# An output projection in scaled fp16 pairs, prepared a block of 256 tokens ahead

## The chip, the cores and the metric

The kernel runs on one core of one Trainium2 chip. The metric is the device time of one execution in microseconds (us).

## What is computed

One hybrid encoder layer is applied to two batches, of 4096 and of 1024 tokens, with a width of 1024. RMSNorm and one combined projection feed three branches (a long convolution through an FFT, dilated attention over three windows, and cross-attention into a memory); the branches are concatenated, gated and projected. The change concerns the last line, and the loads of its weights:

```python
z = h @ w_in                                   # h = rms_norm(x), w_in 1024 x 3584
y_hy  = x0 * (conv + s * skip)                 # 384 channels
y_att = sum over three windows of softmax-weighted outputs   # 384 channels
y_mem = memory_attention(...)                  # 256 channels
mixed = concat([y_hy, y_att, y_mem]) * silu(gate)
return x + mixed @ w_out                       # w_out 1024 x 1024, f32
```

The matrix products want more than one 16-bit or reduced pass: each f32 operand is split into a high and a low part, and three products (high by high, high by low, low by high) are added in PSUM.

## The kernel before, in words

The work is written as one Python class on top of a tile framework. The order on TensorE is the order in which the program issues it; on the other engines (VectorE, ScalarE, GpSimd and the SP queue, which issues all DMAs) the framework's scheduler chooses the order from priorities and dependencies when the kernel is built. Each engine then runs its list in order, so an instruction that waits holds all behind it.

- First the channels of the convolution are projected, and its filter made. Then two streams are woven on TensorE: `dense` projects q, k and v (`qkv`, tile by tile of 128 tokens) and later the gates (`gates`, matmuls `zg`); `side` runs the long convolution, the memory branch and the attention.
- While `qkv` runs its second half it takes one step of the generator `gate_prep` (L1166) before each tile, 18 steps in all. In the kernel before `gate_prep` has eight: each loads 128 columns of the gate's weights into the tile `ws` (one buffer, tag `gws`), scales and splits them with `wsplit`, and stores them to `wgd`. `long_conv` runs meanwhile; its first stage (`conv_stage1`) reads a PSUM tile `a` (two buffers) with ScalarE and VectorE, which write the pair `av` (VectorE's part is L1294); four such pairs make one store `as_d`.
- The output comes last, after the gates. `out_weights` (L1428) loads `w_out` in eight pieces `wos` and splits each into `wo`: a rounded fp32r copy by ScalarE (L1434) and the remainder by VectorE (L1435).
- `output` (L1437) works through 20 blocks of 256 tokens, each of two tiles of 128. `hy(n)` loads the convolution's parts (`hc`, `hs`, `hx`) and the gate `gg` of a block, applies Silu (L1456), the skip (L1459, VectorE) and two products on GpSimd (L1462, L1464) to give `mxh`. `merge(n, t)` loads one tile's three attention outputs `y` (the tile y3, two buffers) and the memory output into `ya` (two buffers), and merges the three by their softmax denominators: small VectorE operations `md` and `mw` (L1483 to L1494), one Exp on ScalarE (L1488), products on VectorE and GpSimd (L1497, L1501), and the sum `ya` (L1504).
- `mixed(k)` (L1512) makes one tile's operand: TensorE transposes `ya` in five pieces into two PSUM tiles `ot` (tag f, three buffers, L1525), VectorE multiplies by the gate into `mm` (L1526), ScalarE rounds `mm` and `mxh` to fp32r into `mhi` (L1529, L1531), and VectorE (L1530) and GpSimd (L1532) subtract to give `mlo`.
- The loop at the end of `output` runs over 40 tiles. Each takes two halves of 512 columns; for each half `mm3` (L277, matmuls at L282 to L284) issues 24 matmuls into the PSUM tile `oo` (two buffers), which VectorE adds to the residual `xr` (L1553). The transposes for tile k+1 stand ahead of tile k's matmuls, `merge` for tile k+2 is issued in the same step.

```python
nc.tensor.matmul(out, pick_l(lh, k), pick_r(rh, k), start=(k == 0), stop=False)
nc.tensor.matmul(out, pick_l(lh, k), pick_r(rl, k), start=False, stop=False)
nc.tensor.matmul(out, pick_l(ll, k), pick_r(rh, k), start=False, stop=(k == n - 1))
```

Of the kernel before, what the change touches and what calls it, by code (L numbers as in the profile page):

```python
# [150 lines left out]
XR = 4  # L151
# [30 lines left out]
class Layer:  # L182
# [983 lines left out]
    def gate_prep(self, pool):  # L1166

        self.wgd = self.dram.tile([P, 8, KC * 2 * P], F16, name="wgd")
        self.Sg = self.const.tile([P, 8], F32, name="Sg")
        for j in range(8):  # L1170
# [3 lines left out]
            yield  # L1174

# [252 lines left out]
    def out_weights(self, pool, lpool):  # L1428
        nc, x = self.nc, self.x
        self.wo = wo = pool.tile([P, KC, 2, DM], F32R, name="wo", bufs=1)  # L1430
        for k in range(KC):
            w = lpool.tile([P, DM], F32, tag="xr", name="wos", bufs=XR)
            self.ld(w, x["w_out"][0][k * P:(k + 1) * P, :])
            nc.scalar.activation(out=wo[:, k, 0], in_=w, func=AF.Copy)  # L1434
            nc.vector.tensor_tensor(out=wo[:, k, 1], in0=w, in1=wo[:, k, 0].bitcast(F32), op=ALU.subtract)  # L1435

    def output(self, lpool, rpool, ps):  # L1437
# [29 lines left out]
        def merge(n, t):  # L1467
# [42 lines left out]
        todo = [(n, t) for n in range(len(blocks)) for t in range(B // P)]  # L1510
        pend = {0: hy(0)}
        ms = {0: merge(0, 0), 1: merge(0, 1)}  # L1512

        def mixed(k):
            n, t = todo[k]
            g, mxh = pend[n]
            ya, xr = ms.pop(k)
            ts = slice(t * P, (t + 1) * P)
            hi = rpool.tile([P, KC, P], F32R, tag="mhi", name="mhi", bufs=2)
            lo = rpool.tile([P, KC, P], F32R, tag="mlo", name="mlo", bufs=2)  # L1520
            mm = rpool.tile([P, 5, P], F32, tag="mm", name="mm", bufs=2)
            for c0, nchunk in ((0, 4), (4, 1)):
                tp = ps.tile([P, 4, P], F32, tag="f", name="ot", bufs=3)
                for c in range(nchunk):
                    nc.tensor.transpose(tp[:, c, :], ya[:, (c0 + c) * P:(c0 + c + 1) * P], self.ident)  # L1525
                nc.vector.tensor_tensor(  # L1526
                    out=mm[:, c0:c0 + nchunk], in0=tp[:, :nchunk], in1=g[:, 3 + c0:3 + c0 + nchunk, ts], op=ALU.mult
                )
            nc.scalar.activation(out=hi[:, 3:8], in_=mm, func=AF.Copy)  # L1529
            nc.vector.tensor_tensor(out=lo[:, 3:8], in0=mm, in1=hi[:, 3:8].bitcast(F32), op=ALU.subtract)  # L1530
# [145 lines left out]
```

## Time and profile before

| | |
|---|---|
| time, median of 3 runs | 3075.26 us (3065.23 to 3078.64) |
| time of the profiled execution | 3081.23 us |
| its span, first to last instruction | 3079.5 us |
| mean granted TensorE clock | 0.973 of full speed |
| TensorE busy | 2780.3 us, 90% |
| VectorE, ScalarE, GpSimd busy | 67%, 54%, 43% |
| share of the DMA engines' time | 73% |
| the output's matmuls `oo` | 1920 matmuls, first at 2593.9 us, last at 3074.8 us |

PE is TensorE, PEld its weight loads, DVE VectorE, ACT ScalarE, POOL GpSimd, SPq the queue of SyncE. All times are from the start of the span. A busy share is no limit by itself: TensorE's matmuls overlap, so their pace is read from the distance of their starts.

### The profile page before, as it was taken

To read this page: it belongs to the slowest core of one execution; us is meant where nothing else is said; L and a number is where in the kernel's file an instruction comes from. 1 tells how busy PE (TensorE), PEld (TensorE's weight loads), DVE (VectorE), ACT (ScalarE), POOL (GpSimd) and SP (SyncE) were. 2 spreads that over 40 slices of the span, in tenths; PEclk is the share of its full clock that TensorE was granted. 3 is DMA by queue.
4 is the path that set the end of the run, shared out by engine and by line. 5 is a ranking of instruction groups with operands and counts; after the bars stand their busy time and mean duration, and the time that the engine had idled before them with its cause. 6 is when DMAs were issued, how large, how long until landed. Compare 5 with 4: busy or idle time off the path is not lost. (4 is left out here: it accounts for less than half of the span.)

```text
span 3079.5 us, 55518 instructions
## 1 busy us (share of the span) xinstructions
PE 2780.3 (90%) x19620; PEld 1727.0 (56%) x19620; DVE 2072.2 (67%) x5239; ACT 1667.0 (54%) x3147; POOL 1338.5 (43%) x1574
## 2 busy tenths in 40 slices
PE   5998888988999997987998999998898899999999
PEld 2444444433544444543456666676666665778877
DVE  7777888788668761463668767676667666766663
ACT  5666666334779863472336666565565564323321
POOL 2336777243246651252424333333243344655551
PEclk9999999999999998998999999999999999999999
DMA  7654444545589866685589999998998979777762
GB/s 221 176 154 148 151 153 147 160 154 189 213 227 241 217 178 178 219 180 135 156 192 261 227 204 229 210 226 177 199 220 195 202 175 309 252 245 256 237 219 103
DMA packets 761953, 610.79 MB, mean 198 GB/s; under 512 B 514814, under 2 KB 702358, under 8 KB 758218
## 3 DMA queue, kind: packets, MB, share of 16 engines
q1 hardware_dynamic: 761674, 607.23, 73.4%
q8 instruction: 155, 2.54, 0.3%
q14 instruction: 124, 1.02, 0.1%
HBM read 289.08 MB, written 200.32 MB: 159 GB/s over the span
## 5 line engine op out<-in xcount | busy, mean ns | idle before, releaser
L1067 ACT ACTIVATE pt<-pt,nm 128x256 f32<-128x256 f32 (+2 forms) x880 | 349.8, 472 | 177.0 <-DVE nm L1065 170.2
L282 PE MATMUL z<-wA,hA 128*128 128x512 f16 (+1 forms) x960 | 353.9, 369 | 35.9 <-DVE vr L476 23.3
L284 PE MATMUL z<-wA,hA 128*128 128x512 f16 (+1 forms) x960 | 353.4, 368 | 0.0
L283 PE MATMUL z<-wA,hA 128*128 128x512 f16 (+1 forms) x960 | 353.1, 368 | 0.0
L1055 DVE CUSTOM_DVE_ANT_0 pt<-s,tab,lsc 128x256 f32<-128x256 f32 (+1 forms) x672 | 277.3, 448 | 84.6 <-PE s L1051 74.6
L282 PE MATMUL zh<-hB,wh 128*128 128x512 f16 x720 | 279.2, 388 | 24.4 <-ACT zb L879 24.2
L283 PE MATMUL zh<-hB,wh 128*128 128x512 f16 x720 | 278.8, 387 | 1.5 <-DVE hB L387 1.5
L284 PE MATMUL zh<-hB,wh 128*128 128x512 f16 x720 | 278.9, 387 | 0.0
L282 PE MATMUL oo<-wo,mhi 128*128 128x512 f32 x640 | 257.2, 402 | 8.9 <-ACT mhi L1531 3.6
L284 PE MATMUL oo<-wo,mlo 128*128 128x512 f32 x640 | 253.9, 397 | 0.3 <-POOL mlo L1532 0.3
L283 PE MATMUL oo<-wo,mhi 128*128 128x512 f32 x640 | 253.8, 396 | 0.0
L282 PE MATMUL zg<-hG,wg 128*128 128x512 f16 x640 | 246.0, 384 | 0.0
L284 PE MATMUL zg<-hG,wg 128*128 128x512 f16 x640 | 245.8, 384 | 0.0
L283 PE MATMUL zg<-hG,wg 128*128 128x512 f16 x640 | 245.7, 384 | 0.0
L1083 POOL CAST hl<-pt 128x256 f16<-128x256 f32 (+1 forms) x212 | 104.7, 508 | 312.0 <-ACT pt L1067 238.2
L1103 DVE TENSOR_TENSOR tl<-tt,th 128x512 f16<-128x512 f32 (+1 forms) x280 | 187.7, 672 | 56.7 <-ACT th L1102 55.2
L1102 ACT ACTIVATE th<-tt 128x512 f16<-128x512 f32 (+1 forms) x280 | 160.1, 574 | 115.0 <-PE yp L1124 55.0
L1048 PE MATMUL s<-kT,qT 128*128 128x256 f16 (+2 forms) x720 | 165.8, 261 | 42.0 <-DVE mx L1055 40.8
L1098 PE MATMUL tt<-ident,pt 128*128 128x128 f32 x1088 | 172.3, 280 | 31.3 <-DVE tl L1103 25.2
L1338 ACT ACTIVATE kt<-kp,rn 64x384 f32<-64x384 f32 x328 | 188.0, 573 | 12.8 <-PE kp L1332 7.6
L1084 POOL TENSOR_TENSOR hl<-pt,hl 128x256 f16<-128x256 f32 (+1 forms) x212 | 191.6, 911 | 6.8
L893 DVE SCALAR_TENSOR_TENSOR u<-zb,cw,u 128x512 f32<-128x512 f32 (+2 forms) x180 | 164.4, 917 | 30.4 <-ACT u L889 27.3
(303 smaller groups left out, 7217.1 us busy)
## 6 DMA issues: line engine op xcount, KB each, us to landing
y<-yc SPq DMA_DIRECT2D x120, 198.0 KB
yc<-y SPq DMA_DIRECT2D x112, 198.0 KB
xt<-in_x SPq DMA_DIRECT2D x40, 512.0 KB
hts<-hB SPq DMA_DIRECT2D x10, 2048.0 KB
hA<-hts SPq DMA_DIRECT2D x40, 512.0 KB
rows<-rw SPq DMA_DIRECT2D x40, 512.0 KB
hG<-hts SPq DMA_DIRECT2D x10, 2048.0 KB
gt<-go SPq DMA_DIRECT2D x80, 256.0 KB
```

The source lines that it names most:

```text
L282: nc.tensor.matmul(out, pick_l(lh, k), pick_r(rh, k), start=(k == 0), stop=False)
L283: nc.tensor.matmul(out, pick_l(lh, k), pick_r(rl, k), start=False, stop=False)
L284: nc.tensor.matmul(out, pick_l(ll, k), pick_r(rh, k), start=False, stop=(k == n - 1))
L893: nc.vector.scalar_tensor_tensor(out=u[:, :w], in0=zb[:, c0 + d:c1 + d], scalar=cw[:, j, tap:tap + 1], in1=u[:, :w], op0=ALU.mult, op1=ALU ...
L1048: nc.tensor.matmul(s[:, a, :W], g["qT"][:, h, qs], g["kT"][:, h, kc:kc + W], start=True, stop=False,)
L1055: nc.vector.tensor_tensor_reduce(out=pt[:, h, :W], in0=s[:, a, :W], in1=zero.to_broadcast([P, NMEM]) if mem else tb[:, h, t0:t0 + W], scal ...
L1067: nc.scalar.activation(out=pt[:, h, :W], in_=pt[:, h, :W], func=AF.Exp, bias=nm[:, h:h + 1])
L1084: nc.gpsimd.tensor_tensor(out=hl[:, 1, :, c], in0=src, in1=hl[:, 0, :, c], op=ALU.subtract)
L1098: nc.tensor.transpose(tt[:, a, ci, :], pt[:, 2 * pr + a, w0:w0 + P], self.ident)
L1102: nc.scalar.activation(out=th[:, :, :n], in_=tt[:, :, :n], func=AF.Copy)
L1103: nc.vector.tensor_tensor(out=tl[:, :, :n], in0=tt[:, :, :n], in1=th[:, :, :n], op=ALU.subtract)
L1338: nc.scalar.activation(out=kt[64 * b:64 * b + 64, a], in_=kp[64 * a:64 * a + 64, :DH], func=AF.Identity, scale=rn[64 * a:64 * a + 64, a * ...
```

## The change

The output's operands become pairs of fp16 values. One power of two scales all of `w_out`, and one scales each block of 256 tokens; the pair is value/scale rounded to fp16, and the remainder in fp16. The sum is scaled back when it is added to the residual. To know the scales, the maximum of `w_out` is taken ahead (in nine more steps of `gate_prep`), and the maximum of a block's operand before it is split, so `mixed` now makes a whole block, one block ahead of its matmuls, and `hy` and `merge` run two blocks ahead.

```diff
-XR = 4
+XR = 8
     def gate_prep(self, pool):
...
+        pk = self.peak(pool, "gws")
+        for j in range(8):
+            w = pool.tile([P, KC, P], F32, tag="gws", name="ws", bufs=1)
+            self.ld(w, self.x["w_out"][0][j * P:(j + 1) * P, :].rearrange("p (k n) -> p k n", n=P))
+            nc.vector.tensor_reduce(
+                out=pk[:, j:j + 1], in_=w, axis=AX.XY, op=ALU.max, apply_absolute_value=True
+            )
+            yield
...
+        pk = self.peaks(pool, pk, "gws")
...
+        nc.vector.reciprocal(self.So[:, 1:2], self.So[:, 0:1])
+        yield
     def out_weights(self, pool, lpool):
-        self.wo = wo = pool.tile([P, KC, 2, DM], F32R, name="wo", bufs=1)
+        self.wo = wo = pool.tile([P, KC, 2, DM], F16, name="wo", bufs=1)
...
-            nc.scalar.activation(out=wo[:, k, 0], in_=w, func=AF.Copy)
-            nc.vector.tensor_tensor(out=wo[:, k, 1], in0=w, in1=wo[:, k, 0].bitcast(F32), op=ALU.subtract)
+            nc.scalar.activation(out=wo[:, k, 0], in_=w, func=AF.Identity, scale=self.So[:, 1:2])
+            nc.vector.scalar_tensor_tensor(
+                out=wo[:, k, 1], in0=w, scalar=self.So[:, 1:2], in1=wo[:, k, 0], op0=ALU.mult, op1=ALU.subtract
+            )
...
-            y3 = pool.tile([P, 3, YW], F32, tag="y3", name="y3", bufs=2)
+            y3 = pool.tile([P, 3, YW], F32, tag="y3", name="y3", bufs=3)
-            ya = pool.tile([P, 640], F32, tag="ya", name="ya", bufs=2)
+            ya = pool.tile([P, 640], F32, tag="ya", name="ya", bufs=4)
...
+        def mixed(n):
+            g, mxh = pend.pop(n)
+            hi = rpool.tile([P, KC, B], F16, tag="mhi", name="mhi", bufs=2)
+            lo = rpool.tile([P, KC, B], F16, tag="mlo", name="mlo", bufs=2)
+            mm = rpool.tile([P, 5, B], F32, tag="mm", name="mm", bufs=1)
+            pk = self.peak(rpool, "mo")
+            nc.vector.tensor_reduce(
+                out=pk[:, 0:1], in_=mxh, axis=AX.XY, op=ALU.max, apply_absolute_value=True
+            )
+            for t in range(NT):
...
+                    tp = ps.tile([P, 4, P], F32, tag="f", name="ot", bufs=3)
+                    for c in range(nchunk):
+                        nc.tensor.transpose(tp[:, c, :], ya[:, (c0 + c) * P:(c0 + c + 1) * P], self.ident)
...
+            nc.vector.tensor_reduce(out=pk[:, 1:2], in_=mm, axis=AX.XY, op=ALU.max, apply_absolute_value=True)
+            nc.vector.tensor_reduce(out=pk[:, 0:1], in_=pk[:, 0:2], axis=AX.X, op=ALU.max)
+            pk = self.peaks(rpool, pk, "mo")
...
+            for c, src in ((slice(3, 8), mm), (slice(0, 3), mxh)):
+                nc.scalar.activation(out=hi[:, c], in_=src, func=AF.Identity, scale=sc[:, 0:1])
+                nc.vector.scalar_tensor_tensor(
+                    out=lo[:, c], in0=src, scalar=sc[:, 0:1], in1=hi[:, c], op0=ALU.mult, op1=ALU.subtract
                 )
...
+        for n, (i, b) in enumerate(blocks):
+            hi, lo, sc = nxt
+            for t in range(NT):
...
+                    if (t, hf) == (0, int(n == 0)) and n + 1 < len(blocks):
+                        nxt = mixed(n + 1)
+                        if n + 2 < len(blocks):
+                            pend[n + 2] = hy(n + 2)
...
+                    nc.vector.scalar_tensor_tensor(
+                        out=xr[:, hf * 512:(hf + 1) * 512], in0=o, scalar=sc[:, 1:2],
+                        in1=xr[:, hf * 512:(hf + 1) * 512], op0=ALU.mult, op1=ALU.add,
+                    )
```

`peaks` takes the maximum over the 128 partitions with two 32x32 transposes, two reductions and seven small copies on VectorE.

Three places show what moved. The lines of the changed kernel are its own: L1553 is its product `mm`, L1593 its addition to `xr`, L1503 to L1524 its `merge`, L1312 its `av`.

TensorE, between two blocks. Before, a tile's five transposes stand between two tiles:

```order
L282 MATMUL oo<-wo,mhi 128x512
L283 MATMUL oo<-wo,mhi 128x512
L284 MATMUL oo<-wo,mlo 128x512
L1525 MATMUL ot<-ident,ya 128x128 x5
L282 MATMUL oo<-wo,mhi 128x512
```

Now the ten of a block stand in one row, every 96 matmuls:

```order
L283 LDWEIGHTS mhi
L283 MATMUL oo<-wo,mhi 128x512
L284 LDWEIGHTS mlo
L284 MATMUL oo<-wo,mlo 128x512
L1552 MATMUL ot<-ident,ya 128x128 x10
L282 LDWEIGHTS mhi
```

The ten write four PSUM tiles `ot`, of which there are three, so the tenth transpose needs the first tile emptied by the first product `mm`.

VectorE in a block of the middle. Before, after the transposes of one tile:

```order
L1553 TENSOR_TENSOR xr<-oo,xr 128x512
L1526 TENSOR_TENSOR mm<-ot,gg 128x512
L1526 TENSOR_TENSOR mm<-ot,gg 128x128
L1504 TENSOR_TENSOR ya<-y_34495 128x384
L1459 SCALAR_TENSOR_TENSOR hc<-hs,skip,hc 128x256 x3
L1530 TENSOR_TENSOR mlo<-mm,mhi 128x640
L1483 TENSOR_TENSOR md<-y_34698 128x6
```

Now, after those of a block, the maximum and the scale come in between, and the low parts (L1568) follow 14 rows later:

```order
L1593 SCALAR_TENSOR_TENSOR xr<-oo,mos,xr 128x512
L1553 TENSOR_TENSOR mm<-ot,gg 128x4x128
L1553 TENSOR_TENSOR mm<-ot,gg 128x128
L1524 TENSOR_TENSOR ya<-y_34187 128x384
L1553 TENSOR_TENSOR mm<-ot,gg 128x4x128
L1553 TENSOR_TENSOR mm<-ot,gg 128x128
L1524 TENSOR_TENSOR ya<-y_34212 128x384
L1557 TENSOR_REDUCE peak<-mm 128x1
L1558 TENSOR_REDUCE peak<-peak 128x1
L222 STREAM_TRANSPOSE peaks<-peak 128x32
L1503 TENSOR_TENSOR md<-y_34431 128x6
L223 TENSOR_REDUCE peak<-peaks 128x1
```

The first `mm` stands behind the addition to `xr` of the block's last half; the waits of `merge` for its loads (L1503) stand within the chain that makes the scale.

The SP queue during `conv_stage1`. Now each load of a piece of `w_out` into the one buffer `ws` stands between two stores `as_d`:

```order
L195 DMA ws<-in_w_out 128x1024
L198 DMA rows_75<-rw 128x2048
L198 DMA as_d_80<-av 128x3072
L195 DMA ws<-in_w_out 128x1024
L198 DMA as_d_80<-av 128x3072
```

On VectorE each piece's maximum then stands behind four `av`:

```order
L1181 TENSOR_REDUCE peak<-ws 128x1
L1312 TENSOR_TENSOR av<-a_6925,av 128x384
L1312 TENSOR_TENSOR av<-a_6939,av 128x384
L1312 TENSOR_TENSOR av<-a_6955,av 128x384
L1312 TENSOR_TENSOR av<-a_6969,av 128x384
L1181 TENSOR_REDUCE peak<-ws 128x1
```

Before, the stores and the `av` followed one another with nothing between.

## Rows read from the trace of the kernel before

**Rows 1.** The page: busy time and share by engine.

```profile
PE 2780.3 (90%) x19620; PEld 1727.0 (56%) x19620; DVE 2072.2 (67%) x5239; ACT 1667.0 (54%) x3147; POOL 1338.5 (43%) x1574
```

**Rows 2.** Stages: length, busy us of each engine, granted clock, DMA share, GB/s.

```profile
800.00:860.00 60.00, 59.90 (x407) 40.39 (x406) 37.91 (x80) 47.24 (x108) 9.15 (x9) 1.00 0.55 207
2550.00:2600.00 50.00, 48.58 (x248) 24.13 (x245) 28.38 (x54) 20.87 (x28) 18.63 (x15) 1.00 0.99 347
2700.00:2937.00 237.00, 234.50 (x1056) 189.58 (x1055) 157.15 (x348) 72.67 (x90) 132.55 (x99) 1.00 0.73 245
```

**Rows 3.** Timeline of PE in the output: start, us, line, operation.

```profile
2701.63 0.40 PE L284 MATMUL oo<-wo,mlo 128*128 128x512 f32 x1
...
2707.93 0.40 PE L284 MATMUL oo<-wo,mlo 128*128 128x512 f32 x1
2708.17 0.71 PE L1525 MATMUL ot<-ident,ya 128*128 128x128 f32 x5
2708.63 0.48 PE L282 MATMUL oo<-wo,mhi 128*128 128x512 f32 x1
2708.95 0.40 PE L283 MATMUL oo<-wo,mhi 128*128 128x512 f32 x1
```

**Rows 4.** Timeline of PE from the gates to the output's first matmuls.

```profile
2559.74 0.38 PE L282 MATMUL zg<-hG,wg 128*128 128x512 f16 x1
...
2591.90 0.38 PE L284 MATMUL zg<-hG,wg 128*128 128x512 f16 x1
2592.11 0.71 PE L1525 MATMUL ot<-ident,ya 128*128 128x128 f32 x5
2593.90 0.50 PE L282 MATMUL oo<-wo,mhi 128*128 128x512 f32 x1 [1.07 <-ACT mhi L1531]
...
2594.98 0.50 PE L284 MATMUL oo<-wo,mlo 128*128 128x512 f32 x1 [0.35 <-POOL mlo L1532]
```

**Rows 5.** The page's groups: busy us, mean ns, idle us before, releaser.

```profile
L282 PE MATMUL oo<-wo,mhi 128*128 128x512 f32 x640 | 257.2, 402 | 8.9 <-ACT mhi L1531 3.6
```

**Rows 6.** Groups of DVE, 2700 to 2937 us, ten blocks: busy, mean ns, idle before.

```profile
L1553 DVE TENSOR_TENSOR xr<-oo,xr 128x512 f32<-128x512 f32 x40 | 27.5, 687 | 11.9 <-PE oo L284 11.9
L1530 DVE TENSOR_TENSOR mlo<-mm,mhi 128x640 fp32r<-128x640 f32 x20 | 20.6, 1029 | 3.2 <-ACT mhi L1529 3.2
L1483 DVE TENSOR_TENSOR md<-y 128x6 f32<-128x6 f32 x20 | 18.1, 905 | 39.3 <-DMA y<-yc 39.3
L1526 DVE TENSOR_TENSOR mm<-ot,gg 128x512 f32<-128x512 f32 x19 | 12.9, 680 | 0.0
```

**Rows 7.** Groups of ACT and POOL, the same ten blocks.

```profile
L1529 ACT ACTIVATE mhi<-mm 128x640 fp32r<-128x640 f32 x20 | 14.8, 740 | 55.1 <-DVE mm L1526 55.1
L1532 POOL TENSOR_TENSOR mlo<-mxh,mhi 128x384 fp32r<-128x384 f32 x20 | 29.3, 1463 | 0.0
```

**Rows 8.** Timelines of DVE and of POOL at 2740 us.

```profile
2741.01 1.79 DVE L1483 TENSOR_TENSOR md<-y 128x6 f32<-128x6 f32 x1
...
2740.43 2.35 POOL L1462 TENSOR_TENSOR hc<-hc,hx 128x768 f32<-128x768 f32 x1 [0.76 <-DMA y<-yc]
```

**Rows 9.** The tile ws (min/median/max ns); timeline of DVE, four small copies.

```profile
L252 DVE TENSOR_REDUCE peak<-ws x32: 1160/1208/1221, 7.8 to 1489.7; 128x1 f32<-128x1024 f32 x32
L265 DVE SCALAR_TENSOR_TENSOR wgp<-ws,wsa,wgp x16: 737/746/2382, 647.0 to 793.2; 128x512 f16<-128x512 f32 x16
...
786.00 0.72 DVE L228 COPY peaks<-peak 32x32 f32<-32x32 f32 x4
```

**Rows 10.** SP's issue of one load of ws, POOL's first use; groups of DVE, 800:860.

```profile
753.86 0.44 SPq L195 DMA_DIRECT2D ws<-in_w_in  x1
...
760.02 1.90 POOL L251 TENSOR_TENSOR ws<-ws,g_in 128x1024 f32<-128x1024 f32 x1 [4.83 <-DMA ws<-in_w_in]
...
L1294 DVE TENSOR_TENSOR av<-a,av 128x384 f16<-128x384 f32 x48 | 26.6, 556 | 21.0 <-ACT av L1293 20.4
```

**Rows 11.** The same for another load of ws.

```profile
693.35 0.46 SPq L195 DMA_DIRECT2D ws<-in_w_in  x1
...
698.02 2.10 POOL L251 TENSOR_TENSOR ws<-ws,g_in 128x1024 f32<-128x1024 f32 x1 [5.03 <-DMA ws<-in_w_in]
```

**Rows 12.** Timeline of PE after an idle stretch, and a window behind it.

```profile
302.62 0.32 PE L733 MATMUL a<-ks,dft 128*128 128x384 f16 x1 [4.01 <-DVE fav L738]
...
304.00:306.00 2.00, 2.00 (x7) 0.73 (x6) 2.00 (x4) 2.00 (x4) 1.00 (x2) 0.50 0.02 5
```

More of the change, by code (lines that the diff above doesn't have):

```diff
@@ L1174, in gate_prep @@
             yield
+        nc = self.nc
+        pk = self.peak(pool, "gws")
[6 more added lines that the diff above has]
+            yield
+        self.So = self.const.tile([P, 4], F32, name="So")
+        nc.vector.tensor_reduce(out=pk[:, 0:1], in_=pk[:, 0:8], axis=AX.X, op=ALU.max)
+        pk = self.peaks(pool, pk, "gws")
+        nc.vector.tensor_scalar_max(self.So[:, 2:3], pk[:, 0:1], 1e-30)
+        self.pow2(self.So[:, 3:4], self.So[:, 2:3])
+        nc.vector.tensor_scalar_mul(self.So[:, 0:1], self.So[:, 3:4], 1.0 / 16.0)
+        nc.vector.reciprocal(self.So[:, 1:2], self.So[:, 0:1])
+        yield
     def gate_fetch(self, step):
@@ L1508, in merge @@
             return ya, xr
[L1510 to L1527, printed above, removed]
-                )
-            nc.scalar.activation(out=hi[:, 3:8], in_=mm, func=AF.Copy)
-            nc.vector.tensor_tensor(out=lo[:, 3:8], in0=mm, in1=hi[:, 3:8].bitcast(F32), op=ALU.subtract)
-            nc.scalar.activation(out=hi[:, 0:3], in_=mxh[:, :, ts], func=AF.Copy)
-            nc.gpsimd.tensor_tensor(out=lo[:, 0:3], in0=mxh[:, :, ts], in1=hi[:, 0:3].bitcast(F32), op=ALU.subtract)
-            return hi, lo, xr
@@ L1535, in output @@
[L1535 to L1557 removed]
+        NT = B // P
@@ new lines, in output @@
+        nxt = mixed(0)
+        for k in range(NT, 2 * NT):
+            ms[k] = merge(*tiles[k])
+        for n, (i, b) in enumerate(blocks):
+            hi, lo, sc = nxt
+            for t in range(NT):
+                _, xr = ms.pop(n * NT + t)
+                ts = slice(t * P, (t + 1) * P)
+                for hf in range(2):
+                    if (t, hf) == (0, int(n == 0)) and n + 1 < len(blocks):
+                        nxt = mixed(n + 1)
+                        if n + 2 < len(blocks):
+                            pend[n + 2] = hy(n + 2)
+                            for k in range((n + 2) * NT, (n + 3) * NT):
+                                ms[k] = merge(*tiles[k])
+                    o = ps.tile([P, 512], F32, tag="d", name="oo", bufs=2)
+                    yield from self.mm3(
+                        o, hi, lo, 0, 1, KC, lambda a, c, ts=ts: a[:, c, ts],
+                        lambda a, c, hf=hf: wo[:, c, a, hf * 512:(hf + 1) * 512],
+                    )
+                    nc.vector.scalar_tensor_tensor(
+                        out=xr[:, hf * 512:(hf + 1) * 512], in0=o, scalar=sc[:, 1:2],
+                        in1=xr[:, hf * 512:(hf + 1) * 512], op0=ALU.mult, op1=ALU.add,
+                    )
+                t0 = b * B + t * P
+                self.st(self.out[i][t0:t0 + P, :], xr)
```

39 lines of the change are left out of this document (16 added, 23 removed).

## The prediction

> **What bounds the kernel now.** I read the busy shares first, then the stages, then TensorE's timeline at the two places that the change touches, then who it waits for. TensorE is busy for 90% of the span, no other engine for over 67% [rows 1]. In the output it is the bound: of 237 us in the middle, ten blocks, it is busy for 234.5 at full clock, VectorE for 157.2, and the DMA engines for 0.73 [rows 2]. So a block takes 23.7 us. The reader should see how even the matmuls' starts are: 27 steps in 6.30 us, 233.3 ns each [rows 3]. Five transposes and the switch back take 0.55 us (from 2707.93 to 2708.95 is 1.02 us, of which 0.47 are two steps), so two tiles make 96 x 0.2333 + 1.1 = 23.5 us, nearly all of the block. Before all 640 matmuls of the first kind only 8.9 us of idle time stand [rows 5]. The other place is the first stage of the long convolution, 800 to 860 us, where `gate_prep` would put its new steps: TensorE is busy for 59.9 of 60 us [rows 2].
>
> **The matmuls.** The gates' matmuls have the new form already, 128x512 in fp16 with fp16 weights: 149 steps in 32.16 us, 215.8 ns [rows 4]. 1920 x 17.5 ns is 33.7 us less. The 200 transposes stay in f32.
>
> **The first block.** Before, TensorE went from the gates' last matmul at 2591.90 to the first low part at 2594.98 [rows 4]. Now the whole chain of a block lies open between them: half a us of transposes; two pairs of products `mm`, 1.6; the maximum of 1280 columns, 1.5 by the 1.21 us for 1024; `peaks` and five scalars, some 16 small instructions at the 0.18 us of a small copy, 3.0; the rounding on ScalarE, twice the 0.74 us for 640 at most; the low parts of 1280 and 768 columns at 0.75 us for 512, 1.9 and 1.1 [rows 6, 7, 9]. That is 11 us. Woven into VectorE's list are three skip products and fifteen small operations of `merge`, 4 to 6 us more, some of which wait for loads in a stretch where the DMA engines are full (0.99, 347 GB/s) [rows 2]. I take 16 us, so useful matmuls from about 2608: 13 us more (9 to 19).
>
> **The clock.** After 4.01 us without a matmul, TensorE's granted clock fell to 0.50 (1.2 GHz) in the window from 304 to 306 us [rows 12]. The gap of the first block is three times as long. One us is lost in that window alone, and its neighbours are not whole; I take 1.7 (0 to 3).
>
> **Every later block: the fourth PSUM tile.** The tenth transpose waits for the first `mm`, which stands behind the last half's `xr`. Counted from the last matmul's start: it ends after 0.38 us, `xr` takes 0.69 and `mm` 0.68, so the tile is free after 1.75; the tenth transpose would have started after some 1.2 (0.22 and nine at 0.11, a fifth of the 0.55) [rows 3, 4, 6]. That leaves 0.6, and a restarted matmul takes 0.50 for 0.38: 0.7 us, 19 times, 13.3 us. A block is then 96 x 0.2158 + 1.1 + 0.7 = 22.5 us.
>
> **VectorE's load.** Per block it had 15.7 us (157.15 over ten). The change adds the two maxima, 0.9 and 1.5; the 16 small ones, 3.0; the low parts, 3.0; nothing that counts at `xr`; and takes away two L1530 of 1.03 [rows 2, 6, 9]. That makes 22.0 of 22.5 us. Before, it could wait for 8 us in a block, 3.9 of them for `y` [rows 6]; now no such wait is hidden. The lower bound is 0 (three `y` buffers and the longer lead end that wait, and GpSimd is rid of two subtractions of 1.46 us [rows 7]); the upper is the 3.9 as before, less the 0.5 that are free, 3.4. I take 0.6 per block, near the lower end, because the extra buffer lets the loads go a tile earlier and the order leaves only two waits for `y` in the chain; 17 blocks (all but the first, and the last two, which prepare less) make 10 us.
>
> The lock: at 2741.01 an operation on six columns took 1.79 us, until GpSimd's product, running since 2740.43, ended at 2742.78 [rows 8]. The Trainium skill, page "SBUF — State Buffer", section "SBUF: two separate sides", gives the rule: VectorE operations with two SBUF inputs and GpSimd share a port pair as an exclusive lock for a whole instruction, and the loser stops fully. The trace agrees here. By the rule the change moves work the wrong way, since both low parts are now such operations on VectorE; if one of them in each block met a product of 2.35 us, 17 blocks would cost 40 us. I count nothing, since in the order GpSimd waits for `mw` while they run; the case is the second rival's.
>
> **The weights' maximum.** The eight loads share one buffer, so they form a loop: load, maximum, next load. From issue to use such a load took 4.7 and 6.2 us [rows 10, 11]; with 1.2 for the maximum [rows 9] and 0.1 for the queue a turn is 6.0 to 7.5. TensorE's order gives it four `av`, 5.0 us (48 in 60 us [rows 10]). VectorE stands at the maximum, `av` behind it, and with both buffers of `a` full TensorE stands too. Seven turns lose 7 to 17 us, less the 2.5 us of two buffers; whole rows of `w_out` may load faster than those columns, then nothing is lost. I take 7 (0 to 18). The split of `wo` by VectorE and ScalarE keeps its size and lies beside the gates: 0.
>
> **The sum.** Of the 8.9 us of waits before [rows 5], the 7.8 behind the first matmul are counted anew above. -33.7 + 13 + 1.7 + 13.3 + 10 + 7 - 7.8 = +3.5 us on a profiled time of 3081.23. That execution is 6 us above the median of the runs, inside their spread of 13; on the median of 3075.26 the forecast is **3079 us, no change that can be told** (about 0.5%, 15 us, is what a measurement of this kernel can tell).
>
> **The rivals.**
> - *TensorE stays the bound, and the new chains hide.* No late VectorE, no loss at the loads, and a first block at the lower end: -33.7 + 9 + 1.7 + 13.3 - 7.8 = -17.5, so 3058 us. For it: the third `y` buffer, two blocks of lead, GpSimd's relief. Against it: VectorE at 22.0 of 22.5. Chance 0.17.
> - *VectorE becomes the bound of every block* (slower). Its place is the list between two products `mm`: the wait for `y` or for GpSimd's lock adds to the 22.0. It decides from 0.5 us of waits in a block; 2.0 us over that, half of the 3.9 us wait of before, and 17 blocks make 34 us instead of 10: +27, 3102 us. For it: every wait of before is still in the list. Against it: the wait arose with two buffers. Chance 0.17.
> - *The loop of loads paces the convolution* (slower). At the longer load, 17 us, and with TensorE idle for two of each seven us its clock falls now and then, 3 more: +16.5, 3092 us. For it: the single buffer. Against it: pieces in whole rows. Chance 0.10.
> - *The matmuls don't speed up*, because the weights' loads or the shape hold them at 233 ns: +37, 3112 us. The gates' 215.8 ns stand against it. Chance 0.02.
>
> **How the numbers follow.** My case has the other 0.54, and its own range is 3062 to 3094. It spills little over the 15 us bound, so faster is the first rival, 0.17; slower is the second, third (just over the bound) and fourth, 0.27 with a little off; the same is 0.56. The range of 3056 to 3103 takes in the first rival and the middle of the second and leaves out the rest of it and the fourth.
>
> **What would show it.** The profile after should have `oo` steps of 0.216 us; a gap of 13 to 16 us before the first of them, with a clock of 0.5 behind it; in each block an idle 0.6 to 0.7 us of TensorE at the transposes, put down to `mm`; VectorE over 90% busy in the middle; between 790 and 860 us waits of VectorE for `ws`, and of TensorE for `av` or `peak`. The forecast is wrong if blocks take under 22 us or over 24, if the first block's chain is hidden under the gates, or if the loop of loads costs more than 18 us.

## The result, and the profile after

The changed kernel takes **3176.81 us**, median of 4 runs (3168.92 to 3179.47), against 3076.65 us (3065.23 to 3078.64, 4 runs) of the kernel before: a ratio of 1.0324, 95% interval 1.0299 to 1.0348. It is slower by 3.2%, 100 us, far outside the range forecast. The last matmul starts at 3168.5 us in the profiled execution, before at 3074.8. So 93.7 us are to be found, and the trace puts them in three places: the gates end 12.9 us later (2604.8 instead of 2591.9), the first block's chain costs 12.5 more, and the blocks of the output take 68.3 more (548.1 us from the first low part to the last matmul, before 479.8), though each matmul became faster.

The page's busy shares, which answer to [rows 1]:

```profile
PE 2781.0 (88%) x19620; PEld 1561.5 (49%) x19620; DVE 2180.0 (69%) x5664; ACT 1658.6 (52%) x3104; POOL 1273.7 (40%) x1534
```

Two windows (length, busy us of PE, PEld, DVE, ACT, POOL, granted clock, DMA share, GB/s): the stretch of [rows 2], and one block of the middle, from one row of transposes to the next.

```profile
2700.00:2937.00 237.00, 196.01 (x874) 89.72 (x872) 168.48 (x456) 57.74 (x60) 82.72 (x66) 0.93 0.60 199
...
2822.13:2851.16 29.03, 23.87 (x107) 10.93 (x106) 20.18 (x56) 6.99 (x7) 10.11 (x9) 0.94 0.60 203
```

Where TensorE was busy for 234.5 of 237 us before, it is now busy for 196.0, at a clock of 0.93. A block takes 29.0 us instead of 23.7, and **no engine is busy for all of it**: in the block shown TensorE is busy for 23.9 us, and VectorE has 20.2 us of work, 70%.

The timeline of PE in that stretch: start, us, line, operation, and in brackets the idle time ahead and what ended it.

```profile
2699.67 0.38 PE L284 MATMUL oo<-wo,mlo 128*128 128x512 f16 x1
...
2708.73 0.38 PE L284 MATMUL oo<-wo,mlo 128*128 128x512 f16 x1
2708.95 1.15 PE L1552 MATMUL ot<-ident,ya 128*128 128x128 f32 x9
2712.36 0.33 PE L1552 MATMUL ot<-ident,ya 128*128 128x128 f32 x1 [2.27 <-DVE mm L1553]
```

The matmuls keep the promise of [rows 4]: 42 steps in 9.06 us, 215.7 ns each. The tenth transpose waits, as foreseen, but for 2.27 us here, where 0.6 was worked out. All waits of TensorE from the end of the gates on (us in total, times, longest):

```profile
PE ot L1552 <- DVE mm L1553: 47.5, 20, 7.4
PE oo L282 <- DVE xr L1593: 28.1, 11, 4.8
PE oo L282 <- ACT mhi L1567: 9.9, 1, 9.9
PE oo L284 <- DVE mlo L1568: 2.8, 1, 2.8
PE oo L282 <- DVE peak L215: 1.5, 3, 0.9
```

Behind the first block's two (`mhi`, `mlo`) all are waits for VectorE: 76.9 us without the 0.24 of the first block. And VectorE itself waited meanwhile, by its own list of waits:

```profile
DVE md L1503 <- DMA y<-yc: 49.4, 23, 4.9
...
DVE md L1504 <- DMA y<-yc: 32.4, 12, 4.0
```

82 us for the attention outputs `y`, which belong to an operand whose matmuls are still two blocks ahead. The timelines of DVE, of SP's queue and of ACT in the block from 2822 to 2851 us show what such waits do. DVE:

```profile
2830.22 0.21 DVE L222 STREAM_TRANSPOSE peaks<-peak 128x32 f32<-128x32 f32 x1
2833.99 0.17 DVE L1503 TENSOR_TENSOR md<-y 128x6 f32<-128x6 f32 x1 [3.56 <-DMA y<-yc]
2834.07 0.18 DVE L223 TENSOR_REDUCE peak<-peaks 128x1 f32<-128x32 f32 x1
...
2840.22 0.17 DVE L1504 TENSOR_TENSOR md<-md,y 128x6 f32<-128x6 f32 x1 [2.93 <-DMA y<-yc]
...
2842.72 1.55 DVE L1568 SCALAR_TENSOR_TENSOR mlo<-mm,mos,mhi 128x1280 f16<-128x1280 f32 x1 [1.23 <-ACT mhi L1567]
...
2851.41 1.44 DVE L1479 SCALAR_TENSOR_TENSOR hc<-hs,skip,hc 128x256 f32<-128x256 f32 x2
```

SP's queue, the same block:

```profile
2824.81 0.37 SPq L195 DMA_DIRECT2D hs<-s_d  x1
2826.94 0.37 SPq L195 DMA_DIRECT2D hx<-x_d  x1
...
2827.94 0.38 SPq L198 DMA_DIRECT2D out<-xr  x1
...
2828.84 2.04 SPq L195 DMA_DIRECT2D y<-yc  x2
2831.01 0.53 SPq L195 DMA_DIRECT2D gg<-gt  x1
2832.68 0.34 SPq L195 DMA_DIRECT2D xr<-in_x  x1
2833.35 2.60 SPq L195 DMA_DIRECT2D y<-yc  x4
```

ACT, the same block:

```profile
2838.23 1.28 ACT L1476 ACT_TABLE_LOAD   x1 [19.72 <-DMA gg<-gt]
2839.52 1.91 ACT L1476 ACTIVATE gg<-gg 128x2048 f32<-128x2048 f32 x1
2841.34 1.35 ACT L1567 ACTIVATE mhi<-mm,mos 128x1280 f16<-128x1280 f32 x1
```

Read the three together. The load of `hs` goes out at 2824.81, when VectorE has finished the skip products that read its buffer (they ran from 2822.38 to 2824.78). Behind it in the queue stand `hx`, a store of `xr`, then two parts of `y`, and behind these the gate `gg` of a later block. The first `y` lands 5 us after its issue, and in VectorE's list `md` stands between two steps of the scale: the reduction L223 stands behind it and waits 3.56 us with it. Two more waits for `y` stand ahead of the low parts: 2.93 us, for a part that stands behind a load of `xr`, and 0.72.

But `y` is not what the low parts wait for last here. That is `mhi` (1.23 us more): ScalarE's list has the Silu of the later gate (L1476, with the load of its table) ahead of this block's rounding (L1567). VectorE had the scale at 2837.3; the gate, issued behind `y`, landed 7.1 us after its issue, at 2838.1, and `mhi` began at 2841.34. Followed back in the trace from 2998 to 2708 us, ten blocks, the chain of what released what goes through a load of `gg` in six blocks (15.3% of the time) and through loads of `y` in three (7.9%).

So the low parts come late, the skip products of the next turn at 2851.41, 29.03 us after the last ones, and the next load of `hs` behind them: **a loop of SP's queue and of the lists of VectorE and ScalarE, and its length is the block**. The DMA engines are not the limit, at a share of 0.60.

The first block, to be held against [rows 4]:

```profile
2604.81 0.38 PE L284 MATMUL zg<-hG,wg 128*128 128x512 f16 x1
...
2616.59 0.61 PE L282 MATMUL oo<-wo,mhi 128*128 128x512 f16 x1 [9.85 <-ACT mhi L1567]
...
2620.43 0.61 PE L284 MATMUL oo<-wo,mlo 128*128 128x512 f16 x1 [2.81 <-DVE mlo L1568]
```

From the last matmul of the gates to the first low part it is 15.6 us, before 3.1.

### The profile page after: what moved, and what is told of

Its sections match the earlier page's. It is cut to its first block, busy times and chain, and to the rows that moved or that the text cites. A ratio compares the mean times of both kernels' runs of the same rounds, so it can differ in the third digit from the quotient of the medians.

```text
span 3173.2 us, 55707 instructions
## 1 busy us (share of the span) xinstructions
PE 2781.0 (88%) x19620; PEld 1561.5 (49%) x19620; DVE 2180.0 (69%) x5664; ACT 1658.6 (52%) x3104; POOL 1273.7 (40%) x1534
## 5 line engine op out<-in xcount | busy, mean ns | idle before, releaser
L282 PE MATMUL z<-wA,hA 128*128 128x512 f16 (+1 forms) x960 | 354.3, 369 | 34.9 <-DVE vr L476 23.9
L282 PE MATMUL zh<-hB,wh 128*128 128x512 f16 x720 | 279.0, 387 | 28.1 <-ACT zb L879 27.9
L282 PE MATMUL oo<-wo,mhi 128*128 128x512 f16 x640 | 254.9, 398 | 39.4 <-DVE xr L1593 28.1
L284 PE MATMUL oo<-wo,mlo 128*128 128x512 f16 x640 | 254.5, 398 | 2.8 <-DVE mlo L1568 2.8
L283 PE MATMUL oo<-wo,mhi 128*128 128x512 f16 x640 | 254.5, 398 | 0.0
```

## The experiments

Each run stands beside runs of the kernel before on the same chip; ratios are to these. The changed kernel is at 1.032. The kernel before took 3074.5 to 3081.1 us on these chips (medians), so a difference in us between runs on different chips is good to some 7 us. Theory 1 says that order costs the time (waits for loads in VectorE's list), theory 2 that the amount of VectorE's work does, theory 3 the fourth PSUM tile.

### One part at a time

**Three resident tiles `y`** (`y_resident`): what of the merges' loads?

```diff
...
-            y3 = pool.tile([P, 3, YW], F32, tag="y3", name="y3", bufs=3)
-            for j in range(3):
-                self.ld(y3[:, j], self.yc[i][j][t0:t0 + P])
+            y3 = ys[(n * (B // P) + t) % 3]
```

> The changed kernel, but only the first three tiles of attention outputs y are loaded, once, and all 40 merges work on these three tiles; so 37 x 3 loads of 198 KB and the waits for them are left out, and with them the right data; every VectorE, ScalarE, GpSimd and TensorE operation stays. Theory 1, late loads: each middle block of 29.0 us holds 7.2 us in which VectorE waits for y, because these loads stand on the SP queue behind loads that wait for VectorE and GpSimd; without them blocks take 22.5 us as at the end of the output, 3080 to 3100 us in all. Theory 2, too much work on VectorE: 20.2 us of busy time and the steps of the scale between them still set the block, 25 us and more, 3125 us or over. Theory 3, the fourth PSUM tile: the wait at the tenth transpose stays at 47 us, 3150 us or over.

3150.3 us, ratio 1.0229 (1.0208 to 1.025). No theory's number. The waits for `y` are gone, but others took their place, as VectorE's list of waits shows:

```profile
DVE mlo L1571 <- ACT mhi L1570: 61.3, 19, 5.0
...
DVE hc L1479 <- DMA hc<-cv: 29.5, 15, 2.9
```

Nine blocks took 25.9 us each on the mean (transposes from 2756.86 to 2989.78). So the loads of `y` are worth about half of the 6.5 us by which a block is above 22.5. The rest is more of the same kind: `mhi` still stands behind the Silu, and loads of `gg` make 24.6% of the chain from 2756 to 2990 us.

**A constant block scale** (`const_block`): the two maxima, `peaks` and the five scalars go, `sc` is set once.

```diff
-            nc.vector.tensor_reduce(out=pk[:, 1:2], in_=mm, axis=AX.XY, op=ALU.max, apply_absolute_value=True)
...
-            nc.vector.tensor_tensor(out=sc[:, 1:2], in0=sc[:, 2:3], in1=self.So[:, 0:1], op=ALU.mult)
+            sc = self.sc
```

> The changed kernel with the constant 1.0 for the scale of a block: the two maxima, peaks and the five scalars of every block are left out, 5.4 us of VectorE's 20.2 us. The operand is still made a block ahead. Theory 1, late loads: the two waits for y in a block stay, but no longer stand within the chain to the operand; VectorE then has some 15 us of work and 7 us of waits, about a block of TensorE, so 3085 to 3120 us, with waits for y of 3 us or more in a block. Theory 2, too much work: blocks of 22.5 us, 3080 to 3095 us, and the waits for y go too. Theory 3, the fourth PSUM tile: 3140 us or over.

3135.21 us, 1.0181 (1.0153 to 1.0209), blocks of 26.9 us (eight from 2777.06 to 2992.14). That lies between the ranges of theories 1 and 3. VectorE has 13.8 us of work in a block (110.4 in the eight) instead of 20.2, and waits longer for `y`, 101.9 us in all where it was 81.8. The larger part:

```profile
DVE md L1503 <- DMA y<-yc: 95.9, 25, 6.2
```

That is against theory 2 alone: a block lost 6.4 us of VectorE's work and became only 2.1 us shorter.

**Five PSUM tiles** (`ot_five`) and **no maximum of w_out** (`no_wmax`):

```diff
-                    tp = ps.tile([P, 4, P], F32, tag="f", name="ot", bufs=3)
+                    tp = ps.tile([P, 4, P], F32, tag="fe"[c0 // 4], name="ot", bufs=3 - c0 // 4)
```

> The changed kernel with the transposes' four-column tiles in the three PSUM buffers as now and the one-column tiles in two more of another tag, so that no transpose waits for the first product mm. Theory 1 and 2: the 47.5 us of TensorE's waits at the tenth transpose are only where a late VectorE shows first; TensorE then waits at the addition to xr instead, and the time is within 15 us of the 3177 of the change. Theory 3: the waits go, 3120 to 3135 us.

3169.72 us, 1.0284 (1.0258 to 1.0311). As expected by theories 1 and 2: no wait at the transposes is left, and TensorE waits for `xr` instead, 64.2 us where it was 28.1.

```diff
-        for j in range(8):
-            w = pool.tile([P, KC, P], F32, tag="gws", name="ws", bufs=1)
...
+        self.nc.vector.memset(self.So[:, 0:1], 2.0 ** -7)
+        self.nc.vector.memset(self.So[:, 1:2], 2.0 ** 7)
```

> The changed kernel without the nine new steps of gate_prep: the scale of w_out is the constant 1/128. Theory: the loop of loads costs the first stage of the long convolution what its first memory projections are later than before, less what they were late already: 5 to 7 us, and up to 12 if the later stages follow, so 3165 to 3172 us; blocks of the output stay at 29 us. Rival: the 12 us by which the gates end later came from elsewhere, and nothing changes (3177).

3166.81 us, 1.0274 (1.0256 to 1.0293): 10.0 us less than the change (15 by the ratios). The gates end at 2593.6 us there. This settles the 12.9 us ahead of the output: the nine steps made 11.2 of them.

### The order of the lists

Now nothing is left out. The framework can queue instructions of an engine behind a given one of it, without any wait (`issue_after`): merge for block n+2 behind the low parts of block n+1 (`merge_behind`), and `hy` behind the high and low parts as well (`all_behind`).

```diff
...
                         if n + 2 < len(blocks):
-                            pend[n + 2] = hy(n + 2)
-                            for k in range((n + 2) * NT, (n + 3) * NT):
-                                ms[k] = merge(*tiles[k])
+                            with self.tc.issue_after(self.last_lo), self.tc.issue_after(self.last_hi):
+                                pend[n + 2] = hy(n + 2)
+                            with self.tc.issue_after(self.last_lo):
+                                for k in range((n + 2) * NT, (n + 3) * NT):
+                                    ms[k] = merge(*tiles[k])
```

> The changed kernel, same instructions and buffers; only the place of merge in VectorE's list is fixed: merge for block n+2 is queued behind the low parts of block n+1, so that its waits for y come last in a block and its loads have a whole block to land. Theory 1, order: VectorE's 20 us of work fit into a block once no wait for y stands in the list, blocks of 22.5 to 23.5 us, 3080 to 3105 us in all, waits for y under 15 us in sum (82 now). Theory 2, amount: with the same 20 us of work and the same chain blocks stay at 25 us or more, 3125 us or over. From the run with three resident tiles y, where other waits took over (ScalarE's high parts, 61 us), a place between the two is likely too: 3105 to 3125 would say that a second wait comes next.

3204.54 us, 1.0395 (1.0354 to 1.0436): worse than the change. Half an order is no order: ScalarE's Exp stood behind the Silu of a gate `gg` that had not landed (ScalarE waited 38.7 us for `gg` from 2700 to 2937 us, VectorE 65.7 us from 2600 us on for `mw`), and the last addition `ya` was now due at once (TensorE waited 85.2 us for it).

> As the run before it, and also Silu (ScalarE) and the skip products (VectorE) of hy for block n+2 are queued behind the high and the low parts of block n+1, so that the chain to the operand never stands behind the load of a gate gg. If the waits for ScalarE's high parts are the second wait, VectorE's wait for them falls below 15 us and blocks are 22.5 us: 3075 to 3090 us. If not, no change against the run before it.

3116.16 us, 1.0105 (1.007 to 1.014): 60 us less than the change with the same instructions, and 88 less than `merge_behind` on the same chip. So the Silu's wait for `gg` and the skip products had to leave the chain as well as the waits for `y`. No wait for `y` is left, and blocks take 24.06 us, not yet the 22.5 expected. What is left in such a block, in the timeline of DVE and then in that of POOL:

```profile
2814.17 1.25 DVE L1504 TENSOR_TENSOR md<-md,y 128x6 f32<-128x6 f32 x2
2815.38 1.89 DVE L1505 TENSOR_TENSOR mw<-md,y 128x18 f32<-128x18 f32 x2
...
2823.65 1.80 DVE L1524 TENSOR_TENSOR ya<-y 128x384 f32<-128x384 f32 x2 [1.72 <-POOL y L1521]
```

```profile
2813.52 1.81 POOL L1482 TENSOR_TENSOR hc<-hc,hx 128x768 f32<-128x768 f32 x1 [13.00 <-DVE md L1503]
2815.41 1.83 POOL L1484 TENSOR_TENSOR mxh<-hc,gg 128x768 f32<-128x768 f32 x1
```

Four small operations take 3.1 us while GpSimd multiplies, and VectorE waits 1.72 us for GpSimd's sum.

The same with the five PSUM tiles of `ot_five` (`all_behind5`):

> As the run before it, with the transposes in five PSUM tiles. Now that VectorE is in time, the fourth PSUM tile should show its own price, 0.7 us in each of 19 blocks: 13 us less than the run before it. If VectorE is still late, no change.

3135.56 us, 1.0167 (1.0121 to 1.0212): 19 us more instead of 13 less. The transposes came earlier, and waited some 2.6 us in a block for `ya` instead of 1.4; the list of VectorE came out otherwise too, with blocks of 24.7 and 26.4 us, 25.5 on the mean. What of the two made it longer was not tried.

Then merge a whole block earlier (`ahead_behind`: n+3 for n+2 in the loop above), the constant scale on top of `all_behind` (`const_behind`), and `all_behind` without GpSimd's two products in `hy` (`no_hy_pool`). The diff is against `all_behind`.

```diff
-            with self.tc.issue_after(self.last_lo):
-                for k in range((n + 2) * NT, (n + 3) * NT):
+            with self.tc.issue_after(self.last_lo):
+                for k in range((n + 3) * NT, (n + 4) * NT):
...
-            nc.gpsimd.tensor_tensor(out=cvt, in0=cvt, in1=x0, op=ALU.mult)
-            mx = pool.tile([P, 3, B], F32, tag="mxh", name="mxh", bufs=1)
-            nc.gpsimd.tensor_tensor(out=mx, in0=cvt, in1=g[:, 0:3], op=ALU.mult)
-            return g, mx
+            return g, cvt
```

> As the run in which merge and hy were queued behind the parts of the next operand (3116 us), with merge one more block ahead, so that its last addition ya is not due at the next transposes. There a block took 24.06 us, of which VectorE waited 1.7 for GpSimd's sum y just ahead of ya, and TensorE for ya. Theory 1, order: with that wait gone blocks are 22.5 to 22.8 us, 3085 to 3100 us. Theory 2, amount: VectorE's 21 us of busy time with its gaps stay above 23.5 us a block, 3105 to 3120 us.

3116.82 us, 1.0117 (1.0094 to 1.014), blocks of 24.08 us. Taken alone this spoke for theory 2. But VectorE still waited 27.6 us for GpSimd's sum: the addition `ya`, now without haste, again stood ahead of the products `mm` in its list.

> As the run in which merge and hy were queued behind the parts of the next operand (3116 us), with the constant 1.0 as the scale of a block, so without the maxima, peaks and five scalars. Theory 1 and 2 together (order first, then amount): VectorE has 15.5 us of work and no wait for loads, TensorE is the bound, blocks 22.5 us, and the first block's chain is 5 us shorter: 3075 to 3090 us. If blocks stay over 24 us, order and amount together do not explain the loss.

3073.17 us, 0.9989 (0.997 to 1.0008), blocks of 22.49 us. Order first, then amount, takes away the whole loss.

> The run at 3116 us (merge and hy behind) without GpSimd's two products in hy: the convolution's part of the operand is then not multiplied by x0 and by its gate. Nothing else is left out. There VectorE's four small operations of merge that run beside these products took 3.1 us instead of some 0.7, so 2.4 us of a block should go if GpSimd holds VectorE up, and VectorE then waits 1.7 us for GpSimd's sum or less, since GpSimd starts no later: blocks 22.5 to 23 us, 3080 to 3095 us. Rival: the small operations are slow for another reason, blocks stay at 24 us, 3110 us or over.

3100.88 us, 1.0079 (1.0054 to 1.0104), blocks of 23.59 us: 0.47 us less, where 1.1 to 1.6 were expected (15 us in all by the medians, 8 by the ratios). DVE's timeline in a block:

```profile
2808.56 0.23 DVE L1501 TENSOR_TENSOR md<-md,y 128x6 f32<-128x6 f32 x2
2808.75 0.27 DVE L1502 TENSOR_TENSOR mw<-md,y 128x18 f32<-128x18 f32 x2
2810.55 0.30 DVE L1506 TENSOR_TENSOR md<-mw,y 128x18 f32<-128x18 f32 x2 [1.54 <-ACT mw L1505]
...
2816.72 1.80 DVE L1521 TENSOR_TENSOR ya<-y 128x384 f32<-128x384 f32 x2 [2.58 <-POOL y L1518]
```

The four small operations fall from 3.1 to 0.5 us, so GpSimd's products did hold VectorE up; but VectorE only came earlier to its waits for Exp and for GpSimd's sum.

**The full order** (`full_order`) decides. The last addition is a step of its own and stands behind the *next* block's low parts; `y` has four buffers.

```diff
...
+                        with self.tc.issue_after(self.last_lo), self.tc.issue_after(self.last_hi):
+                            if n + 2 < len(blocks):
+                                for k in range((n + 2) * NT, (n + 3) * NT):
+                                    add(k)
+                                pend[n + 2] = hy(n + 2)
+                            if n + 3 < len(blocks):
+                                for k in range((n + 3) * NT, (n + 4) * NT):
+                                    ms[k] = merge(*tiles[k])
```

> All instructions and scales of the change, only their places moved: the last addition ya of a merge stands behind the next block's low parts, ahead of the next merge (y in four buffers), so that VectorE's list holds no instruction that waits for a late load or for GpSimd; the merges of the first two blocks come ahead of the first operand. In the two runs with a block of 24.06 us VectorE waited 1.5 to 1.7 us of it for GpSimd's sum. Theory 1, order alone: 21 to 22 us of VectorE's work fit, blocks 22.5 to 22.8 us, 3080 to 3097 us. Theory 2, the amount is already over TensorE's block: blocks stay at 23.5 us or more, 3105 to 3120 us.

3078.15 us, 1.0017 (1.0002 to 1.0032): 99 us less than the change (94 by the ratios), with all its instructions and scales. One of its blocks (a window as above), then its PE timeline at a row of transposes, and the longest of VectorE's waits from 2700 to 2937 us:

```profile
2785.50:2807.99 22.49, 22.03 (x107) 10.52 (x106) 20.12 (x55) 7.10 (x7) 9.42 (x10) 1.00 0.79 265
```

```profile
2807.99 1.15 PE L1559 MATMUL ot<-ident,ya 128*128 128x128 f32 x9
2809.60 0.33 PE L1559 MATMUL ot<-ident,ya 128*128 128x128 f32 x1 [0.46 <-DVE mm L1560]
```

```profile
DVE xr L1605 <- PE oo L284: 9.2, 10, 0.9
```

VectorE has 20.12 us of work in a block, as it had in the change's 29 us, and the block is 22.49 us; what VectorE waits for longest is now TensorE. ScalarE's Silu now stands behind `mhi`. Theory 1 stands, theory 2 falls: the amount fits, if nothing in the lists waits for late loads. The fourth buffer of `y` was not tried by itself; with three and no wait for `y`, `all_behind` stayed at 24.06 us.

**The maximum of w_out later** (`full_order_late`): in `out_weights`, over the pieces that it loads.

> As the run with the full order, with the maximum of w_out taken in out_weights, from the eight pieces loaded there anyway, instead of in gate_prep. The loop of loads cost 10 us in the pair with and without it (3167 against 3177); here eight maxima and the scale, 14 us of VectorE, stand ahead of the split, beside the gates. If the gates hide them: 8 to 12 us less than the run with the full order. If they delay the first operand: no gain or up to 10 us more.

```diff
+            nc.vector.tensor_reduce(out=pk[:, k:k + 1], in_=w, axis=AX.X, op=ALU.max, apply_absolute_value=True)
+            ws.append(w)
```

3081.96 us, 1.0012 (0.9993 to 1.003): no gain. The convolution got its time back (its first `kp` at 874.1 us instead of 881.7), but the gates ended no earlier (a wait of 5.5 us for `go` stands near their end), and the first operand came later.

### The tile by tile form, and the best versions

**The kernel before with fp16 pairs** (`pairs_by_tile`), its output's order as it was:

> The kernel before, tile by tile as it was, with its operands as fp16 pairs and constant scales (1 for the operand, 1/128 for w_out); no maxima, nothing prepared a block ahead. Theory: 1920 matmuls at 216 instead of 233 ns are worth 34 us and nothing else moves: 3040 to 3052 us. Rival: with blocks of 22.0 instead of 23.7 us the waits for y and for VectorE that were hidden come out: 3060 to 3080 us.

```diff
-            hi = rpool.tile([P, KC, P], F32R, tag="mhi", name="mhi", bufs=2)
+            hi = rpool.tile([P, KC, P], F16, tag="mhi", name="mhi", bufs=2)
```

3081.85 us, 1.0 (0.998 to 1.002): the faster matmuls alone gain nothing. Of its waits in the output, the longest of PE and of DVE:

```profile
PE oo L282 <- DVE xr L1555: 26.3, 21, 4.1
```

```profile
DVE md L1485 <- DMA y<-yc: 81.5, 24, 5.5
```

The kernel before had such waits for `y` too, 66.8 us in the same stretch (39.3 of them in the ten blocks of [rows 6]), and its slower matmuls covered them: its TensorE waited for 8.9 us [rows 5].

Then both tile by tile kernels with an order (`tile_behind` the pairs, `before_behind` the f32 form):

```diff
-            if k + 2 < len(todo):
-                ms[k + 2] = merge(*todo[k + 2])
...
+                    with self.tc.issue_after(self.last_lo), self.tc.issue_after(self.last_hi):
+                        if t == 0 and n + 2 < len(blocks):
+                            pend[n + 2] = hy(n + 2)
+                        if k + 3 < len(todo):
+                            ms[k + 3] = merge(*todo[k + 3])
```

> The fp16 pairs with constant scales in the tile by tile form (3082 us, no gain), with merge a tile and hy half a block further ahead and both queued behind the next tile's parts, y and ya in three buffers, xr in six. Theory: there the faster matmuls were given back as 26 us of TensorE's waits for xr, behind VectorE's waits for y (82 us); with these out of the list blocks are 21.9 us and the gain of 34 us shows, 3042 to 3060 us. Rival: VectorE is too busy even so, 3070 us or over.

> A control: the kernel before, f32 pairs, with only the order of the run beside it (merge and hy further ahead and behind, y and ya in three buffers, xr in five). Before, a block of 23.7 us had 23.5 us of matmuls and transposes, and all waits of TensorE for VectorE came to 9 us: so the order alone is worth 0 to 8 us there, 3073 to 3085 us. If it gains over 15 us, the order was a loss in the kernel before too.

3106.45 us, 1.0091 (1.0069 to 1.0113), and 3160.15 us, 1.0252 (1.0224 to 1.028): both misses. The order that I gave tile by tile left the addition `ya` free, and it went ahead of the low parts, to wait for GpSimd there (124 us in 36 waits and 129 us in 38), as in this row of DVE's timeline of `before_behind`:

```profile
2823.47 1.35 DVE L1504 TENSOR_TENSOR ya<-y 128x384 f32<-128x384 f32 x1 [6.83 <-POOL y L1501]
```

They tell nothing of the fp16 pairs. Nor is all of the 80 us of `before_behind` the price of such rows: 44 us are two waits of TensorE for `ya` at the start of the output, 34.8 and 9.5.

Last, the edits that had paid, together: `const_behind` with `no_wmax` (`const_behind_nw`), and the five PSUM tiles of `ot_five` in `full_order` (`full_order5`) and in that one (`const_behind_nw5`).

> The run with merge and hy behind and a constant block scale (3073 us, blocks of 22.5 us), also with a constant scale for w_out, so without the nine steps of gate_prep: 8 to 12 us less, 3061 to 3066 us, which would be faster than the kernel before by some 0.5%.

3057.55 us, 0.9944 (0.9924 to 0.9965): 4 us below the range expected.

> The run with the full order (3078 us, all scales kept), with the ten transposes of a block in five PSUM tiles. There the tenth transpose waits 0.46 us for the first product mm in each of 17 blocks of 22.49 us. Theory: that is the whole price of the fourth tile now, 8 to 10 us, so blocks of 22.0 us and 3067 to 3071 us, faster than the kernel before by 0.2 to 0.4%. Rival, from the pair with and without the five tiles at 3116 and 3136 us: the earlier transposes only wait for something else, no change or more.

> The run with constant scales and merge and hy behind (3058 us), with the transposes in five PSUM tiles: the same 8 to 10 us, 3047 to 3051 us. Rival: its last addition ya, which stands just ahead of the transposes' products, comes due 0.5 us earlier, and TensorE waits for it instead: no change or more.

3068.65 us, **0.9961** (0.9943 to 0.9978), and 3056.31 us, **0.9911** (0.9885 to 0.9937). The first, as expected, keeps all scales and is 0.4% below the kernel before, whose own executions spread from 3066.7 to 3090.6 there; its blocks take 21.81 us (transposes at 2736.15, 2757.96 and 2779.77), and TensorE waits for nothing at the transposes. The second missed its range: 1 us less than `const_behind_nw` by the medians, and by the ratios the intervals overlap. Its constants were chosen for these inputs.

## Why the prediction was wrong

**Right:** the matmuls (216 ns forecast, 215.7 found; 33.7 us less). The first block (13 us more forecast, 12.5 found, with the clock at half behind it). The loop of loads (7 us, 0 to 18, forecast; 10.0 by the pair with and without it). The steady block of a TensorE that is not held up: 22.5 us forecast, 22.49 in `full_order` and at the end of the changed kernel's own output; the tenth transpose's wait was 0.46 there for the 0.6 worked out. VectorE's work (22.0 us forecast, 20.2 found). Without the 10 us for `y` the forecast's sum is -6.5 us. `full_order`, which has no waits for `y` in its blocks, lies 5 us above the kernel before by its ratio, 10 of them two early waits at the transposes (4.6 and 5.8). That its 3078 us lie beside the 3079 forecast is in part chance.

**Wrong:** the step "VectorE's load", which gave 10 us: "I take 0.6 per block, near the lower end, because the extra buffer lets the loads go a tile earlier and the order leaves only two waits for `y` in the chain". In the block shown three waits for `y` stood ahead of the low parts, of 7.2 us together, not 0.6, and outside the upper bound of 3.4 as well. That bound took the 3.9 us of before as the most that a wait for `y` can be. The runs showed otherwise: the wait is no constant that a third buffer shortens. Loads that stand in SP's queue behind loads which wait for VectorE come later as VectorE comes later; with less work for VectorE the same waits grew (`const_block`), and with an order that gives the loads a block to land they were nil (`all_behind`).

The same step put nothing for ScalarE. It looked for waits in VectorE's list alone, while in ScalarE's list the Silu of a later gate stood ahead of `mhi`. In six of ten blocks the chain ran through that gate's load; with no loads of `y` left blocks were still 25.9 us (`y_resident`), and moving `merge` alone made the time longer (`merge_behind`). The forecast's sign of a late VectorE, over 90% busy in the middle, did not come either: it was 71%, the rest being waits.

The sum of the blocks shows the size. 1920 matmuls at 0.2158 make 414.3 us and 19 rows of transposes 20.9. Of the 548.1 us measured, 76.9 are waits of TensorE, where 13.3 + 10 were planned, and the remaining 36.0 are nearly all the clock (the slow steps between matmuls, added one by one, make 32), where 1.7 was planned, behind the first gap alone. The second rival named half of this mechanism, with its place (the list between two products `mm`) and its point (0.5 us of waits in a block); its price of 34 us left out that a late VectorE delays its own loads, ScalarE's list, and the clock.

**The lock** was counted at nothing. The kernel before paid it too (`md` of six columns took 905 ns on the mean [rows 6]), and `no_hy_pool` prices it: 2.6 us of VectorE's time in a block, though only 0.47 us of the block, on the small operations of `merge`, not on the low parts that the rival had in mind. The Trainium skill, page "SBUF — State Buffer", section "SBUF: two separate sides", tells of the exclusive lock between VectorE's operations on two SBUF inputs and GpSimd; these rows agree. It wasn't the cause: in `full_order` the same four operations still take 3.1 us, and the block is 22.49 us.

What the profile of before did show was this: VectorE's waits for `y` were in the list, 39.3 us in ten blocks [rows 6], and TensorE's block of 23.7 us hid them. The Trainium skill, page "PSUM — Partial Sum Buffer", section "Engine vs sequencer instructions", says that the queues of ScalarE, VectorE and GpSimd are strictly first in, first out. The trace agrees (the 3.56 us of the reduction L223 behind `md`, and `mhi` behind the Silu), and it is the sentence from which the forecast should have started: what stands in the chain's list ahead of a step of the chain holds it up, whichever block it belongs to.

## What to carry to other kernels

Before a change makes an engine's slack small, list every instruction of that engine that waits for a load or for another engine, and what stands behind it; a wait that was hidden then comes out, and where the load's queue waits for the same engine it grows into a loop. Do the same for every engine that the chain passes, as ScalarE here. In a list that a scheduler made from assumed landing times, pin work that is not due behind the chain that is, on every engine that takes part and for the last step too: here half of the order was worse than none (3205 us), and all of it was worth some 95 us. The faster matmuls were worth nothing until the next engines' waits were out of the lists.

## What the hardware showed that was not expected

The clock made about a third of the blocks' loss. The tenth transpose of the block above came after a wait of 3.29 us, and the granted clock fell just behind it. The timeline of PE, and a window of 4 us:

```profile
2826.56 0.33 PE L1552 MATMUL ot<-ident,ya 128*128 128x128 f32 x1 [3.29 <-DVE mm L1553]
...
2827.33 0.63 PE L284 MATMUL oo<-wo,mlo 128*128 128x512 f16 x1
2827.76 0.63 PE L282 MATMUL oo<-wo,mhi 128*128 128x512 f16 x1
```

```profile
2826.00:2830.00 4.00, 3.44 (x10) 1.38 (x11) 4.00 (x7) 0.00 (x0) 2.19 (x2) 0.62 0.71 217
```

Steps are 0.43 us, at 1.2 GHz, until 2830.3, some eight of them: 1.7 us on top of 3.29. But the same wait a block later cost nothing more; the steps behind it are 0.22 us at once:

```profile
2855.60 0.33 PE L1552 MATMUL ot<-ident,ya 128*128 128x128 f32 x1 [3.29 <-DVE mm L1553]
2855.76 0.38 PE L282 MATMUL oo<-wo,mhi 128*128 128x512 f16 x1
2855.98 0.38 PE L283 MATMUL oo<-wo,mhi 128*128 128x512 f16 x1
```

A block earlier, at 2797.52, thirteen slow steps followed a wait of 3.29 us. After the 2.27 us at 2712.36 there were none, after 2.60 us at 2758.41 there were nine. So no single price of a wait can be read from these rows; over the whole output 76.9 us of waits came with some 36 us of low clock, half as much again.
